# Starting attention inside the last gate pair, and taking bias and gate weights ready-made from DRAM

## The chip, the cores and the metric

The kernel runs on one core of a Trainium2 chip. The metric is the device time of one execution in microseconds, as the median over several runs. The engines are TensorE (PE, with its weight loads shown as PEld), VectorE (DVE), ScalarE (ACT), GpSimd (POOL), and SyncE (SP), whose queue issues every DMA of this kernel.

## The reference

One layer of a hybrid encoder on 1024 rows of width 1024, all in float32:

```
h  = x @ w_in                                   # q, k, v for two head groups, and two gates
ya = chunk_band_attention(qa, ka, va, rel_bias) @ w_proj_a   # 8 softmax heads, band of 9 chunks
yb = stick_breaking_attention(qb, kb, vb) @ w_proj_b         # 8 heads, sigmoid and running products
mix = (sigmoid(ga + b_gate_a) * ya + sigmoid(gb + b_gate_b) * yb) @ w_out
x = layer_norm(alpha * x + mix)
g, u = split(x @ w_ffn_in)
x = layer_norm(alpha * x + (silu(g) * u) @ w_ffn_out)
```

In the softmax heads a score gets a bias that depends on the clipped distance of row and column: on a block of 128 rows by 640 columns, every row has the same list of values, shifted by one place from row to row ("skewed").

## The kernel before

Every float32 factor is split into a high and a low part of a faster matmul type (`split`: a ScalarE cast, then a VectorE subtraction), and a product is three matmuls: high by high, high by low, low by high. A tile is 128 x 1024; its store or load moves 512 KB.

**The order of work.** First the plain products of pair 0 and gate 10. Then the *pairs*: two 128-column blocks of `w_in` are multiplied together by a scheme of seven half-size products (`pair_steps`, each 12 matmuls of 128 x 512). Pairs 1 to 7 give q and k and store them to DRAM; then comes the v stage; then pairs 8 to 12 give ten of the sixteen gates, apply the sigmoid and store them (`out_g`). `run_pairs` walks through the seven steps j = 0 to 6 of each pair, and after a step loads and prepares the weights of later pairs (`right`, `left`) and calls `also`, where side work is placed by hand: the operands of the later output projection (`wo_right`, twelve parts of loads, sums, splits and stores) and the split of the y projection's weights (`proj_weights`), all kept in DRAM until needed.

Then **attention**: 16 heads (0 to 7 softmax, 8 to 15 stick-breaking) with eight rows of blocks each. A row is scores on TensorE into a `sc` bank, then VectorE, ScalarE and GpSimd on the weights (`soft_block`, `stick_block`); later a value step transposes them (`turn`), splits them, and multiplies by v (`mult`). `LEAD` says how many rows are begun ahead of each value step; the first six rows of head 0 begin before its first value step. Between these steps *fillers* keep TensorE busy (`fill_all`, `FILL` per head): the 48 matmuls each of gates 11 to 15, then the 192 of the products yA = y x w_proj_a. Gates 12 to 15 have their weights loaded and split at that time (`load_gate`, cast on ScalarE, subtraction on GpSimd at line 557). While gate 15 runs, `load_y` loads y0 to y3, high and low, into `xt` tiles that held x's parts `xh` and `xl`. Gate 15 takes first all eight k for the low half of the rows, then all eight for the high half. Gates 11 to 15 get their sigmoid only when they are read back (`reload_gate`).

`small_inputs` writes the reversed and padded bias table to `rel_dr`; `rel_bias_tile` reads it skewed into a tile and negates and reverses it on ScalarE (line 652).

After attention come the yB products, the output projection, the norm, and the feed-forward part in the same seven-product scheme.

**What sets the order of instructions.** A scheduler orders each engine's instructions by program order and by when it expects them to be ready, so a filler that is ready may stand ahead of work that waits for a load. Each engine then runs its list strictly in that order. Tiles come from small groups: `cycle(QK, ...)` takes `qs`, `kh` and `kl` in turn, two tiles each (six in all), which also hold q and k of the heads; `gt` has 3, `kp` 4, `op` 8, `xt` 16. Banks: `mm` 2, `sc` 2, `tr` 3, `pv` 1.

Of the kernel before, what the change touches and what calls it, by code (L numbers as in the profile page):

```python
# [18 lines left out]
P = 128  # L19
# [31 lines left out]
def hybrid_trunk_kernel(ctx: ExitStack, tc, x, xt, w_in, w_v, b_gate, rel_bias, w_proj,  # L51
# [54 lines left out]
    pa_dr = [[dr.tile([P, 1024], F32, name=f"pa_dr{i}{p}") for p in "hl"] for i in range(4)]  # L106
    left_dr = {(p, i): dr.tile([P, HW], F32, name=f"left_dr{p}_{i}")
               for i in range(NP2) for p in ORDER}
    rel_dr = dr.tile([8, 896], F32, name="rel_dr")
# [72 lines left out]
    def pair_steps(nm, W, ops, c, done, xtag="mm"):  # L182


        st = {}

        def begin(key, tag, p):
            st[key] = bank(tag, f"{key}{nm}")
            product(st[key], W, ops, p, True)

        def add(dst, src):
            nc.vector.tensor_tensor(dst, src, dst, ALU.add)  # L192

        def p1():
            begin("sx", xtag, 1)
            nc.scalar.copy(c("11"), st["sx"])

        def p2():
            begin("sy", "sc", 2)
            add(c("11"), st["sy"])  # L200
            done("11", None)

        def p6():
            product(st["sx"], W, ops, 6, False)
# [138 lines left out]
    def project(i):  # L343
        kind, pair = work[i][:2]
        tl = {}

        def tile_of(side):
            if side not in tl:
                tl[side] = cycle(QK, f"c{side}_{i}")
# [14 lines left out]
        def out_g(side):  # L364
            gate_sigmoid(tl[side], 2 * pair + int(side) - 1)
# [10 lines left out]

        return pair_steps(f"p{i}", Wa[i], ops_x, c, done)

    def run_pairs(lo, hi, first, also):
# [150 lines left out]

    def proj_weights(cc):

        raw = cycle(QK, f"pa_raw{cc}", F32R)
        hi = cycle(QK, f"pa_hi{cc}", F32R)
        for j, cs in enumerate((LO, HI)):
            load_then(raw[:, cs].bitcast(F32), w_proj[2 * cc + j][:, 0:HW])
        split(hi, raw, raw.bitcast(F32))
        for d, t in zip(pa_dr[cc], (hi, raw)):
            dma(d, t.bitcast(F32))
# [24 lines left out]

    def gate(i, w, gt=None):
# [16 lines left out]
    for _ in gate(first_gate, gate_w, cycle(QK, "gate0")):  # L582
        pass
    first_gate += 1
    wo_at = {(4, 6): 0, (5, 6): 1, (6, 6): 2, (8, 2): 3, (8, 6): 4, (9, 2): 5, (9, 6): 6,
             (10, 2): 7, (10, 6): 8, (11, 2): 9, (11, 6): 10, (12, 2): 11}

    def also(i, j):
# [4 lines left out]
        if i > N_QK and j == 4:  # L593
            proj_weights(i - N_QK - 1)
# [6 lines left out]
    run_pairs(N_QK, len(work), 0, also)  # L601
    first_w = load_gate(first_gate, nc.vector)
# [43 lines left out]
    def rel_bias_tile(head):  # L646
        braw = slot("kp", f"braw{head}")
        src = rel_dr[head:head + 1, 0:640]
        dma(braw[:, 0:640],
            bass.AP(tensor=src.tensor, offset=src.offset, ap=[[1, P], [1, 640]]))  # L650
        bias = slot("kp", f"bias{head}")
        nc.scalar.activation(bias[:, 0:640], braw[:, 0:640][:, ::-1], AF.Copy, scale=-1.0)  # L652
# [150 lines left out]
    def load_proj(cc):  # L803

        parts = []
        for p, d in zip("hl", pa_dr[cc]):
            t = slot("op", f"w{p}_y{cc}", F32R)
            dma(t.bitcast(F32), d)
            parts.append(t)
        return parts  # L810


# [53 lines left out]
    load_qk(heads[0])  # L866
    load_qk(heads[1])
    load_v(heads[0])
    for hd, hidx, g, st, pos, box in vsteps:
# [5 lines left out]
        def begin_rows():  # L875
            begun = state.setdefault("rows", 0)
            upto = min(hidx * 8 + LEAD[hd["br"]][pos], len(wunits))
            for n in range(begun, upto):
                wunits[n]()
            state["rows"] = max(begun, upto)  # L880

        if pos == hidx == 0:
            begin_rows()
# [4 lines left out]
        begin_rows()  # L888
# [493 lines left out]
```

## Time and profile before

| | us |
|---|---|
| median of three runs | 1431.96 (1430.93, 1431.96, 1436.22) |
| profiled execution | 1438.71 |
| its span, first to last instruction | 1436.9 |
| TensorE busy in it | 1405.3 |
| VectorE, ScalarE, GpSimd busy | 1024.1, 689.4, 309.9 |
| q and k pairs | about 43 to 182 |
| v stage | about 182 to 253 |
| gate pairs 8 to 12 | about 253 to 349 |
| first scores of head 0, of head 8 | 356.9, about 472 |
| yA's first products | 549.5 |

Times in the trace are microseconds from the start of the span. A busy TensorE is counted with the tail of each matmul: one of 128 x 512 shows as about 0.39 us, while in a stream they start about 0.23 us apart; so gaps under some 0.17 us do not show as idle. The page's list of DMAs gives bytes and time to landing. The waits list names what ended the idle time of an engine.

### The profile page before, as it was taken

Reading aid. Unit: us, or ns where it says so; the run is one execution under the profiler, and the core shown is the slowest. Engines: PE = TensorE matmul, PEld = TensorE weight load, DVE = VectorE, ACT = ScalarE, POOL = GpSimd, SP = SyncE. Lnnn points to the kernel's source line nnn. Section 1 sums busy time; section 2 is a strip of 40 time slices with the busy share of each in tenths; the row PEclk is TensorE's granted clock in tenths of the full one; section 3 lists DMA queues with packets and bytes.
Section 4 is the critical chain, followed back from the end, with each engine's and each line's share of the span. In section 5 each row is a group of like instructions: output and inputs, shape, how many; then the busy total and the mean of one; then the engine's idle time right before and its main releaser. Section 6 shows DMA issues by size and latency. Waiting matters only on the chain.

```text
span 1436.9 us, 18884 instructions
## 1 busy us (share of the span) xinstructions
PE 1405.3 (98%) x6592; PEld 1159.7 (81%) x6592; DVE 1024.1 (71%) x1596; ACT 689.4 (48%) x1203; POOL 309.9 (22%) x365
## 2 busy tenths in 40 slices
PE   8999999999999998999999999999999999999997
PEld 6888888888778787888888878888888888888886
DVE  8866467773887987897779995555555544785996
ACT  6444354554888876783233543333333332444540
POOL 0000000000565775771303031111111100300012
PEclk9999999999999999999999999999999999999999
DMA  7565737888787559888862143223322227853521
GB/s 249 169 179 181 234 91 275 300 320 302 201 234 226 168 161 278 269 269 301 312 236 85 69 139 125 94 104 110 110 87 91 95 100 251 316 192 110 174 81 73
DMA packets 102895, 264.49 MB, mean 184 GB/s; under 512 B 10880, under 2 KB 27264, under 8 KB 102800
## 3 DMA queue, kind: packets, MB, share of 16 engines
q1 hardware_dynamic: 102800, 263.29, 55.3%
q8 instruction: 52, 0.85, 0.2%
q14 instruction: 43, 0.35, 0.1%
HBM read 172.25 MB, written 90.99 MB: 183 GB/s over the span
## 4 chain that ended last, share of the span: by engine, by line
PE 83%; DVE 8%; DMA 3%; ACT 3%; issue 2%; POOL 1%; POOLq 0%; SPq 0%; DVEq 0%; ACTq 0%
PE dn L1275 15%; PE sxf L179 14%; PE sxp L179 8%; PE szf L179 6%; PE v L431 5%; PE ops L1134 5%; PE szp L179 4%; PE gps L572 4%; PE syf L179 4%; PE yAps L793 2%; PE syp L179 2%; PE tp_b L730 2%; PE tp_a L730 1%; DMA wRf<-in_w_ffn_in_dram 1%; DMA yh<-y_dr2h 1%
## 5 line engine op out<-in xcount | busy, mean ns | idle before, releaser
L1275 PE MATMUL dn<-dr,dl 128*128 128x512 f32 x924 | 209.6, 389 | 0.0
L1275 PEld LDWEIGHTS dn<-dr,dl 128*128 128x128 f32 x924 | 173.4, 188 | 36.0
L704 POOL TENSOR_TENSOR w_b<-w_b,kp_b 128x511 f32<-128x511 f32 (+3 forms) x96 | 103.8, 1085 | 53.0 <-DVE kp_b L701 49.5
L701 DVE TENSOR_TENSOR_SCAN kp_b<-kp_b,ident_ps 128x512 f32<-128x512 f32 (+3 forms) x96 | 92.7, 966 | 4.0 <-ACT kp_b L699 1.4
L112 ACT CAST dl<-raw 128x512 fp32r<-128x512 f32 x77 | 47.5, 623 | 84.7 <-PE dn L1275 68.6
L1134 PE MATMUL ops<-wr,wl 128*128 128x512 f32 x336 | 78.8, 392 | 0.0
L971 POOL TENSOR_TENSOR mv<-mv,neghalf 128x1 f32<-128x1 f32 x16 | 25.6, 1603 | 242.0 <-DVE mv L970 242.0
L1134 PEld LDWEIGHTS ops<-wr,wl 128*128 128x128 f32 x336 | 62.5, 188 | 12.5
L653 POOL MEMSET bias<- 64x64 f32 x8 | 1.2, 146 | 330.1 <-ACT bias L652 330.1
L113 DVE TENSOR_TENSOR dl<-raw,dl 128x512 fp32r<-128x512 f32 x77 | 53.3, 699 | 24.8 <-ACT dl L112 24.2
L674 POOL TENSOR_SCALAR w_a<-w_a,st_a 128x640 f32<-128x640 f32 (+2 forms) x64 | 46.6, 734 | 75.9 <-PE sc_a L634 38.5
L113 DVE TENSOR_TENSOR pt_b<-tp_b,pt_b 128x512 fp32r<-128x512 f32 (+1 forms) x80 | 49.9, 630 | 16.7 <-ACT pt_b L112 15.8
L112 ACT CAST pt_b<-tp_b 128x512 fp32r<-128x512 f32 (+1 forms) x80 | 44.2, 554 | 36.6 <-PE tp_b L730 36.2
L1072 POOL TENSOR_TENSOR sb<-h 128x512 f32<-128x512 f32 x10 | 20.2, 2021 | 185.6 <-PE syf L179 135.1
L179 PE MATMUL szf<-x1S63h,wcf 128*128 128x512 f32 x168 | 55.1, 389 | 0.0
L192 DVE TENSOR_TENSOR gt<-sxf,gt 128x512 f32<-128x512 f32 x21 | 14.4, 686 | 54.9 <-PE sxf L179 54.9
L671 ACT ACTIVATE w_a<-w_a,st_a 128x640 f32<-128x640 f32 (+2 forms) x64 | 44.7, 699 | 13.2 <-DVE st_a L666 11.8
L699 ACT ACTIVATE kp_b<-sc_b 128x512 f32<-128x512 f32 (+3 forms) x96 | 49.0, 511 | 1.5 <-PE sc_b L634 1.4
L700 ACT ACTIVATE w_b<-sc_b 128x511 f32<-128x511 f32 (+3 forms) x96 | 49.1, 512 | 0.0
L1073 POOL TENSOR_TENSOR sa<-h,h 128x512 f32<-128x512 f32 x10 | 15.9, 1586 | 143.0 <-PE sxf L179 120.3
L730 PEld LDWEIGHTS tp_b<-ident,w_b 128*128 128x128 f32 x288 | 36.6, 141 | 12.1 <-issue 1.0
L730 PE MATMUL tp_a<-ident,w_a 128*128 128x128 f32 x240 | 41.9, 277 | 4.4 <-POOL w_a L674 2.5
(1525 smaller groups left out, 4188.2 us busy)
## 6 DMA issues: line engine op xcount, KB each, us to landing
raw<-left_dr SPq DMA_DIRECT2D x77, 256.0 KB, 2.9
wo_dr<-wo SPq DMA_DIRECT2D x28, 512.0 KB, 3.9
wr<-wo_dr SPq DMA_DIRECT2D x28, 512.0 KB, 8.7
wLf<-in_w_ffn_in_dram SPq DMA_DIRECT2D x22, 512.0 KB, 4.4
wRf<-in_w_ffn_in_dram SPq DMA_DIRECT2D x22, 512.0 KB, 4.3
rows<-in_w_ffn_out_dram SPq DMA_DIRECT2D x22, 512.0 KB, 6.3
left_dr<-h SPq DMA_DIRECT2D x33, 256.0 KB, 2.0
v_dr<-vst SPq DMA_DIRECT2D x16, 512.0 KB, 3.2
```

The costliest lines, as they stand in the source:

```text
L112: nc.scalar.copy(dst_h, src)
L113: nc.vector.tensor_tensor(dst_l, src, dst_h.bitcast(F32), ALU.subtract)
L179: mm(acc, lw[:, ks], rx, start=(first and kt == i == 0), stop=(kt == 3 and i == 2), skip_group_check=not first)
L431: mm(banks[mt], xs[lw][:, ms], o[:, rx], start=(fresh and kt == n == 0), stop=(kt == 3 and n == 2), skip_group_check=not fresh)
L572: mm(acc, lw[:, ks], rx[k][:, cs], start=(k == j == 0), stop=(k == KT - 1 and j == 2))
L699: nc.scalar.activation(kp[:, c0:e], sc[:, 0:n], AF.Sigmoid, scale=-1.0)
L700: nc.scalar.activation(be[:, m0:e], sc[:, m0 - c0:n], AF.Sigmoid)
L701: nc.vector.tensor_tensor_scan(kp[:, c0:e], kp[:, c0:e], ident_ps()[:, 0:n], kp[:, c0 - 1:c0] if c0 else 0.0, ALU.mult, ALU.bypass if c0 e ...
L704: nc.gpsimd.tensor_tensor(be[:, m0:e], be[:, m0:e], kp[:, m0 - 1:e - 1], ALU.mult)
L730: tr(tp[:, j:j + P], wt[qb - q0][:, (kb - qb) * P:(kb - qb + 1) * P], ident)
L1134: mm(acc, lw, rx, start=(fresh and n == m == 0), stop=(n == 3 and m == 2), skip_group_check=not fresh)
L1275: mm(acc, lw, rx, start=(fresh and steps[s][1] == n == 0), stop=(last and n == 2), skip_group_check=not fresh)
```

## The change

- *The last gate pair* (pair 12, `final`) leaves `run_pairs` and stands at the start of attention. Its product 2 moves to the sixth place, its bank for that product from `sc` to `tr`, its result tiles from the q/k tiles to `gt`; its two gates (8 and 9) are stored without sigmoid and get it in `reload_gate`. After its step 0 gate 11's weights are loaded, after step 1 q and k of head 0; rows 0 to 2 of head 0 begin after step 4, rows 3 and 4 after step 5, row 5 after step 6.
- *The side work* of the gate pairs is placed anew, so that all of it stands within pairs 8 to 11.
- *The weights of gates 12 to 15* are split during pairs 3 to 6 and kept in DRAM; attention loads the two parts.
- *The bias*: `small_inputs` writes a negated table and from it eight DRAM tables of 128 equal rows; a head's tile is one skewed read, with no ScalarE step, and one `kp` tile in place of two.
- *Gate 15* takes each k through both halves, in two banks at once, and y0 to y3 are loaded after its matmuls 7, 13, 19 and 25, not 28, 31, 34 and 37.

```diff
-    def pair_steps(nm, W, ops, c, done, xtag="mm"):
+    def pair_steps(nm, W, ops, c, done, xtag="mm", ytag="sc", p2_at=1):
...
-            begin("sy", "sc", 2)
+            begin("sy", ytag, 2)
...
-        return [p1, p2, p6, p5, p7, p3, p4]
+        order = [p1, p6, p5, p7, p3, p4]
+        order.insert(p2_at, p2)
+        return order
...
-        nc.vector.tensor_copy(rel_sb[:, 383:896], rel_in[:, ::-1])
-        nc.vector.tensor_copy(rel_sb[:, 0:383], rel_in[:, 512:513].to_broadcast([8, 383]))
+        nc.vector.tensor_scalar(rel_sb[:, 0:384], rel_in[:, 129:513], -1.0, None, ALU.mult)
+        nc.vector.tensor_copy(rel_sb[:, 384:768], rel_sb[:, 383:384].to_broadcast([8, 384]))
         dma(rel_dr, rel_sb)
+        for head in range(8):
+            src = rel_dr[head:head + 1, :]
+            dma(skew_dr[head], bass.AP(tensor=src.tensor, offset=src.offset,
+                                       ap=[[0, P], [1, 768]]))
...
+                tl[side] = slot("gt", name) if final else cycle(QK, name)
...
-            gate_sigmoid(tl[side], 2 * pair + int(side) - 1)
+            if not final:
+                gate_sigmoid(tl[side], 2 * pair + int(side) - 1)
...
+        if final:
+            return pair_steps(f"p{i}", Wa[i], ops_x, c, done, ytag="tr", p2_at=5)
...
+    def keep_split(name, parts, dst):
+        raw = cycle(QK, f"raw_{name}", F32R)
+        hi = cycle(QK, f"hi_{name}", F32R)
+        for cs, src in parts:
+            load_then(raw[:, cs].bitcast(F32), src)
+        split(hi, raw, raw.bitcast(F32))
+        for d, t in zip(dst, (hi, raw)):
+            dma(d, t.bitcast(F32))
+    def gate_weights(i):
+        keep_split(f"g{i}", [(slice(0, D), gate_src(i))], gw_dr[i])
+    def load_split(name, src):
+        parts = []
+        for p, d in zip("hl", src):
+            t = slot("op", f"w{p}_{name}", F32R)
+            dma(t.bitcast(F32), d)
+            parts.append(t)
+        return parts
...
+    def last_gate(i, w):
+        gt = slot("gt", f"gate{i}")
+        accs = [bank("mm", f"gps{i}_{hf}") for hf in range(2)]
+        for k in range(KT):
+            ks = slice(k * P, (k + 1) * P)
+            for acc, cs in zip(accs, (LO, HI)):
+                for j, (lw, rx) in enumerate(((w[0], xh), (w[0], xl), (w[1], xh))):
+                    mm(acc, lw[:, ks], rx[k][:, cs], start=(k == j == 0),
+                       stop=(k == KT - 1 and j == 2))
+                    yield 1.0
+        for acc, cs in zip(accs, (LO, HI)):
+            nc.scalar.copy(gt[:, cs], acc)
+        dma(g_dr[i], gt)
...
-    wo_at = {(4, 6): 0, (5, 6): 1, (6, 6): 2, (8, 2): 3, (8, 6): 4, (9, 2): 5, (9, 6): 6,
-             (10, 2): 7, (10, 6): 8, (11, 2): 9, (11, 6): 10, (12, 2): 11}
+    wo_at = {(4, 6): 0, (5, 6): 1, (6, 6): 2, (8, 0): 3, (8, 3): 4, (8, 6): 5, (9, 2): 6,
+             (9, 5): 7, (10, 1): 8, (10, 4): 9, (11, 0): 10, (11, 3): 11}
+    pa_at = {(8, 5): 0, (9, 4): 1, (10, 2): 2, (10, 6): 3}
...
-        if i > N_QK and j == 4:
-            proj_weights(i - N_QK - 1)
+        if (i, j) in pa_at:
+            proj_weights(pa_at[i, j])
+        if 3 <= i < 7 and j == 4:
+            gate_weights(i + 9)
...
-    run_pairs(N_QK, len(work), 0, also)
-    first_w = load_gate(first_gate, nc.vector)
+    final = len(work) - 1
+    run_pairs(N_QK, final, 0, also, 1)
...
-        braw = slot("kp", f"braw{head}")
-        src = rel_dr[head:head + 1, 0:640]
-        dma(braw[:, 0:640],
-            bass.AP(tensor=src.tensor, offset=src.offset, ap=[[1, P], [1, 640]]))
         bias = slot("kp", f"bias{head}")
-        nc.scalar.activation(bias[:, 0:640], braw[:, 0:640][:, ::-1], AF.Copy, scale=-1.0)
+        src = skew_dr[head][0:1, 127:767]
+        dma(bias[:, 0:640],
+            bass.AP(tensor=src.tensor, offset=src.offset, ap=[[767, P], [1, 640]]))
...
-            nxt = load_gate(i + 1, nc.gpsimd) if i < 15 else load_proj(0)
-            for n, unit in enumerate(gate(i, w)):
-                if i == 15 and n in (28, 31, 34, 37):
-                    load_y((28, 31, 34, 37).index(n))
+            nxt = load_split(f"g{i + 1}", gw_dr[i + 1]) if i < 15 else load_split("y0", pa_dr[0])
+            for n, unit in enumerate(gate(i, w) if i < 15 else last_gate(i, w)):
+                if i == 15 and n in (7, 13, 19, 25):
+                    load_y((7, 13, 19, 25).index(n))
...
-        if 2 * c + br >= 2 * N_GATE:
+        if 2 * c + br >= 2 * N_GATE - 2:
             gate_sigmoid(t, 2 * c + br)
...
-    load_qk(heads[0])
+    for j, step in enumerate(project(final)):
+        step()
+        also(final, j)
+        if j == 0:
+            first_w.extend(load_gate(first_gate, nc.vector))
+        if j == 1:
+            load_qk(heads[0])
+        if j >= 4:
+            rows_to((3, 5, 6)[j - 4])
     load_qk(heads[1])
     load_v(heads[0])
```

More of the change, by code (lines that the diff above doesn't have):

```diff
@@ L106, in hybrid_trunk_kernel @@
     pa_dr = [[dr.tile([P, 1024], F32, name=f"pa_dr{i}{p}") for p in "hl"] for i in range(4)]
+    gw_dr = {i: [dr.tile([P, 1024], F32, name=f"gw_dr{i}{p}") for p in "hl"]
+             for i in range(12, 16)}
     left_dr = {(p, i): dr.tile([P, HW], F32, name=f"left_dr{p}_{i}")
                for i in range(NP2) for p in ORDER}
-    rel_dr = dr.tile([8, 896], F32, name="rel_dr")
+    rel_dr = dr.tile([8, 768], F32, name="rel_dr")
+    skew_dr = [dr.tile([P, 768], F32, name=f"skew_dr{i}") for i in range(8)]
     def split(dst_h, dst_l, src):
@@ L344, in project @@
         kind, pair = work[i][:2]
+        final = i == len(work) - 1
         tl = {}
@@ L348, in tile_of @@
             if side not in tl:
-                tl[side] = cycle(QK, f"c{side}_{i}")
+                name = f"c{side}_{i}"
+                tl[side] = slot("gt", name) if final else cycle(QK, name)
             return tl[side]
@@ L375, in done, with run_pairs @@
                 out("2")
+        if final:
+            return pair_steps(f"p{i}", Wa[i], ops_x, c, done, ytag="tr", p2_at=5)
         return pair_steps(f"p{i}", Wa[i], ops_x, c, done)
-    def run_pairs(lo, hi, first, also):
+    def run_pairs(lo, hi, first, also, ahead=0):
         steps = {i: project(i) for i in range(lo, hi)}
@@ L387, in run_pairs @@
                 p()
-                if j == 0 and i + 1 < hi:
+                if j == 0 and i + 1 < hi + ahead:
                     right(i + 1)
-                if j == 1 and lo + 2 <= i + 2 < hi and i + 2 >= lo + first:
+                if j == 1 and lo + 2 <= i + 2 < hi + ahead and i + 2 >= lo + first:
                     left(i + 2)
@@ L529, in wo_right @@
             put(4, b[:, LO])
-    def proj_weights(cc):
[L533 to L539, printed above, removed]
+    def keep_split(name, parts, dst):
[6 more added lines that the diff above has]
+            dma(d, t.bitcast(F32))
+    def proj_weights(cc):
+        keep_split(f"pa{cc}", [(cs, w_proj[2 * cc + j][:, 0:HW])
+                               for j, cs in enumerate((LO, HI))], pa_dr[cc])
+    def gate_weights(i):
[7 more added lines that the diff above has]
+        return parts
     def load_w(srcs, name, raw, hl, lo_eng):
@@ L768, in value_steps @@
         return steps
+    first_w = []
     def fill_all():
@@ L780, in fill_all @@
         for cc in range(4):
-            nxt = load_proj(cc + 1) if cc < 3 else None
+            nxt = load_split(f"y{cc + 1}", pa_dr[cc + 1]) if cc < 3 else None
             if cc:
@@ L801, in fill_all @@
             w = nxt
[L803 to L810, printed above, removed]
     KEEP, kept = 5, {}
@@ L865, in hybrid_trunk_kernel, with rows_to @@
     goal = 0.0
-    load_qk(heads[0])
+    def rows_to(upto):
+        for n in range(state.get("rows", 0), upto):
+            wunits[n]()
+        state["rows"] = max(state.get("rows", 0), upto)
+    for j, step in enumerate(project(final)):
[7 more added lines that the diff above has]
+            rows_to((3, 5, 6)[j - 4])
     load_qk(heads[1])
@@ L874, in hybrid_trunk_kernel @@
             load_v(heads[hidx + 1])
[L875 to L883, printed above, removed]
         if st == 0:
@@ L887, in hybrid_trunk_kernel @@
         turn()
-        begin_rows()
+        rows_to(min(hidx * 8 + LEAD[hd["br"]][pos], len(wunits)))
         last = goal
```

2 lines of the change are left out of this document (1 added, 1 removed).

## The prediction

> **What bounds the kernel now.** I read the page first (its busy times and clock), then the stages as windows, then the waits of TensorE, then the timeline and the chain of waits where TensorE stops.
>
> ```profile
> PE 1405.3 (98%) x6592; PEld 1159.7 (81%) x6592; DVE 1024.1 (71%) x1596; ACT 689.4 (48%) x1203; POOL 309.9 (22%) x365
> ```
>
> TensorE is the bound, and no matmul is added or taken away. The span is 1436.9 us, so at most 31.6 us (1436.9 - 1405.3) of plain idle time can be won, plus slow-clock time and short gaps that count as busy.
>
> ```profile
> 43.00:182.00 139.00, 139.00 (x612) 114.11 (x611) 87.21 (x112) 60.02 (x82) 0.00 (x0) 1.00 0.65 195
> 253.00:329.00 76.00, 75.76 (x334) 62.40 (x333) 54.07 (x74) 43.87 (x62) 0.29 (x2) 1.00 0.84 305
> 329.00:349.00 20.00, 20.00 (x90) 16.53 (x90) 7.47 (x10) 9.41 (x13) 0.00 (x0) 1.00 0.89 331
> 355.00:380.00 25.00, 22.02 (x124) 17.17 (x123) 16.75 (x64) 17.67 (x39) 11.33 (x18) 1.00 0.79 215
> 380.00:476.00 96.00, 92.55 (x569) 77.00 (x568) 81.00 (x261) 81.17 (x188) 54.73 (x88) 1.00 0.75 214
> 535.00:550.00 15.00, 15.00 (x86) 12.85 (x85) 13.66 (x17) 12.86 (x30) 11.96 (x22) 1.00 1.01 304
> 550.00:565.00 15.00, 10.13 (x48) 8.41 (x47) 7.59 (x10) 6.58 (x16) 4.77 (x6) 0.77 1.00 328
> ```
>
> The columns are busy us and count of TensorE, its weight loads, VectorE, ScalarE and GpSimd, then clock, DMA share, GB/s. The pair stages (43 to 182, 253 to 349) lose nothing, so whatever the change puts there is free only as long as that holds. The change aims at three losing stretches: the start of attention (355 to 380), the softmax heads (380 to 476), and 550 to 565, where the clock falls as well.
>
> **Part 1: y's loads.** Gate 15 runs just before the yA products, which need y0 to y3 (eight transfers of 512 KB).
>
> ```profile
> 538.73 0.38 SPq L819 DMA_DIRECT2D yh<-y_dr0h  x1
> 540.64 0.35 SPq L819 DMA_DIRECT2D yl<-y_dr1l  x1
> ...
> 549.70 0.32 SPq L819 DMA_DIRECT2D yl<-y_dr3l  x1
> ...
> SPq L819 <- DMA yh<-y_dr1h: 2.6, 1, 2.6
> ...
> 525.00:530.00 5.00, 5.00 (x31) 4.28 (x30) 4.37 (x6) 3.50 (x9) 3.46 (x7) 1.00 0.10 38
> 530.00:535.00 5.00, 5.00 (x31) 4.34 (x30) 3.76 (x6) 3.87 (x10) 2.87 (x3) 1.00 0.32 86
> ...
> 526.82 0.40 PE L572 MATMUL gps<-xl,wh_g 128*128 128x512 f32 x1
> ...
> 536.44 0.39 PE L572 MATMUL gps<-xl,wh_g 128*128 128x512 f32 x1
> ...
> 542.71 0.40 PE L572 MATMUL gps<-xh,wl_g 128*128 128x512 f32 x1
> ...
> 553.61 0.33 PE L744 MATMUL pv_b<-pt_b,v 128*128 128x256 f32 x1
> 558.64 0.80 PE L793 MATMUL yAps<-yh,wh_y 128*128 128x512 f32 x1 [4.70 <-DMA yh<-y_dr2h]
> ...
> 562.01 0.63 PE L793 MATMUL yAps<-yl,wh_y 128*128 128x512 f32 x1
> 562.44 0.55 PE L793 MATMUL yAps<-yh,wl_y 128*128 128x512 f32 x1
> 562.82 0.39 PE L793 MATMUL yAps<-yh,wh_y 128*128 128x512 f32 x1
> 563.05 0.39 PE L793 MATMUL yAps<-yl,wh_y 128*128 128x512 f32 x1
> ```
>
> The y loads can start only when gate 15's second half lets x's tiles go, and then crowd into 11 us with the DMAs already at share 1.01; SP even waits for the first of them to land before it issues the last. The first yA products run, and the seventh waits 4.70 us for y2h. Then matmuls start 0.43 us apart (562.01, 562.44), where 0.23 is the pace (562.82, 563.05). From 558.64 to 562.82, 4.2 us at about half speed cost 2.1. Together 6.8 us.
>
> After, gate 15 takes each k through both halves, so each xh/xl pair falls free every 6 matmuls. Do the loads at its matmuls 7, 13, 19, 25 find free tiles? Were tiles reused strictly in turn, y1l would take xh3, which the row at 542.71 still reads; it issued at 540.64. So a load takes whichever tile fell free first, and eight are free by matmul 24. The matmuls numbered 7 and 25 ran at 526.82 and 536.44, so the loads issue between 527 and 537, over 12 us earlier than the last one did (549.70), into a stretch in which the DMAs moved 38 and 86 GB/s. Value: **-6.8**, bounds -7.5 and -3 (the reload of gA, or head 12's q and k in the same queue, could become the late one). Gate 15 now holds both `mm` banks at once; at its ends a copy of 0.6 us stands close to the next use: counted below.
>
> The Trainium skill ("TensorE: Matmul & The Clock Gate", Part 1) says the clock is halved after an idle window of some 3.4 us; the rows at 562 agree (0.43 against 0.23). By its rule a leftover wait under 3.4 us would cost only itself.
>
> **Part 2: the start of attention.**
>
> ```profile
> 340.54 2.72 PE sxp L179 x12
> ...
> 348.70 8.39 PE gps L572 x37
> ...
> PE tp_a L730 <- POOL w_a L674: 1.6, 3, 1.1
> PE tp_a L730 <- DVE pt_a L113: 0.8, 1, 0.8
> ...
> 345.57 0.89 SPq L617 DMA_DIRECT2D kl<-k_dr  x1
> ...
> 351.39 0.84 SPq L617 DMA_DIRECT2D kl<-k_dr  x1
> ...
> 356.92 0.45 PE L633 MATMUL sc_a<-kh,qs 128*128 128x320 f32 x2
> ```
>
> While q and k of head 0 are on their way (its k loads stand from 345.57 to 351.39, the first score at 356.92), TensorE uses up 37 of gate 11's 48 filler matmuls; when the rows start there is little left to fill with, and 355 to 380 loses 25 - 22.02 = 2.98 us idle. At the later pace (569 in 96 us, 0.169 us each) 25 us would hold 148 matmuls, not 124: 4.0 us short. After, q and k load during the last pair, whose c tiles no longer sit in their slots, rows 0 to 5 run over its products 2 and 4 (5.4 us), and the 37 matmuls fill heads 0 to 2. Value **-2.5**, bounds 0 (the gaps move on with the next rows) and -4.
>
> What it puts into the last pair: ten score cuts of two matmuls. If TensorE's order keeps the first six together, two banks at VectorE's pace hold it: about 0.6 us a cut (486 ns, in the group below, plus its read-out) against 0.3 of matmuls, some 2 us at most; before, matmuls of the gate were mixed between the scores. With the bank changes of gate 15 and two gates' sigmoids moved to their reload (1.15 us of ScalarE each, L341 below): **+0.5**, bounds 0 and +2.5.
>
> **Part 3: prepared bias and weights.** It takes out of the softmax heads:
>
> ```profile
> L652 ACT ACTIVATE bias<-braw 128x640 f32<-128x640 f32 x7 | 5.2, 741 | 0.9 <-DMA braw<-rel_dr 0.9
> L548 ACT CAST wh_g<-wr_g 128x1024 fp32r<-128x1024 f32 x3 | 3.1, 1049 | 0.2 <-DMA wr_g<-in_w_in_dram 0.2
> L557 POOL TENSOR_TENSOR wl_g<-wr_g,wh_g 128x256 fp32r<-128x256 f32 x12 | 9.4, 820 | 0.3 <-ACT wh_g L548 0.3
> L666 DVE CUSTOM_DVE_ANT_0 w_a<-sc_a,bias 128x320 f32<-128x320 f32 (+2 forms) x64 | 31.0, 486 | 19.2 <-PE sc_a L634 15.3 <-POOL bias L654 3.2 <-PE sc_a L633 0.2
> ```
>
> 8.3 us of ScalarE, 9.4 of GpSimd, 3.2 of VectorE's waits for a bias. None of it is TensorE's own time; the stage loses 96 - 92.55 = 3.45 us idle to such chains, in gaps of well under 1 us, and more in gaps too short to show. Value **-2.0**, bounds 0 and -5. The bias tile now waits for its DMA without ScalarE between; that drops 0.74 us, and one `kp` slot of two, a head.
>
> The work comes back in pairs 3 to 6: four times a cast and a subtraction as these,
>
> ```profile
> L113 DVE TENSOR_TENSOR pa_raw<-pa_raw,pa_hi 128x1024 fp32r<-128x1024 f32 x4 | 4.9, 1218 | 0.3 <-ACT pa_hi L112 0.3
> ...
> L341 ACT ACTIVATE c<-c,bg 128x1024 f32<-128x1024 f32 x9 | 10.4, 1154 | 5.2 <-DVE c L192 5.1
> ...
> L112 ACT CAST pa_hi<-pa_raw 128x1024 fp32r<-128x1024 f32 x4 | 4.2, 1048 | 0.7 <-DMA pa_raw<-in_w_proj_dram 0.7
> ```
>
> (pa_raw and pa_hi; the row between them is a gate's sigmoid) beside 87 and 60 busy us of 139: hidden. Its DMA is 4 x 1.57 MB, and the eight skewed tables write 8 x 0.39 MB: 9.4 MB on 27 MB (195 GB/s x 139 us), a share of 0.65 rising to about 0.88. What queues behind the eight table writes on SP is q and k stores, whose tiles ScalarE needs, and weight loads with a pair (19 us) in hand. **+0.3**, bounds 0 and +3.
>
> **Part 4: the gate pairs.** All remaining w_out parts and w_proj splits move ahead of the last pair, into pairs 8 to 11. In transfers of 524 KB: a pair needs 4 (two weight loads, two gate stores); a w_out part 4, 3 or 2; a w_proj split 3. Pair 8: 4+4+3+3+2 = 16, or 8.39 MB; pair 9: 14, 7.34; pair 10: 16, 8.39; pair 11, which loads one weight tile fewer: 8, 4.19. Together 28.3 MB in 4 x 7 x 2.72 = 76.2 us, 371 GB/s. Before, 305 at a share of 0.84 and 331 at 0.89 put a full share at 363 to 372. At 368, pairs 8 and 10 need 22.8 us each for their 19.0, pair 9 19.9: 8.5 us behind at the end of pair 10, of which pair 11 (11.4 for 19.0) makes up most.
>
> ```profile
> 272.00:291.00 19.00, 18.76 (x83) 15.17 (x82) 13.46 (x19) 11.17 (x16) 0.00 (x0) 1.00 0.90 332
> ...
> 277.47 6.02 DMA woraw<-in_w_out_dram
> ```
>
> Behind a late w_out or w_proj load stand ScalarE and VectorE, in order, and behind them the copies that free a bank: TensorE has two to five products (5.4 to 13.6 us) before it stops. A 6.02 us wait cost 0.24 us (19 - 18.76). With 8.5 against 5.4, 3 us at one place; I take **+2.0**, bounds 0 and +8.5. The Trainium skill ("DMA: Bandwidth & Descriptors", Specifications) gives some 358 GB/s from HBM to a core. By that figure 28.3 MB take 79.1 us, an estimate that speaks against the change; the 363 to 372 drawn from the trace lies just above it.
>
> **Sum:** -6.8 - 2.5 + 0.5 - 2.0 + 0.3 + 2.0 = **-8.5 us**. The profiled execution took 1438.71 us (span 1436.9 and 1.8 around it), so 1430.2 by it; it is 6.75 us above the median of the three runs, 1431.96, and I carry the difference over whole: **1423.5 us**. About 0.5% (7.2 us: 1424.8 to 1439.1) is what a measurement of this kernel tells from no change.
>
> **Rivals.**
> A. *As summed*: 1419 to 1429, chance 0.52, of which 0.10 lies above 1424.8.
> B. *The gate pairs become DMA-bound* (slower). If the DMAs carry no more than the 305 GB/s which 253 to 329 moved, 28.3 MB take 92.8 us in place of 76.2, 16.6 us late; with the other terms (-10.5) that is +6.1, 1438. Below 301 GB/s (17.7 us late) it ends slower by over 0.5%, at 1440 or more. For it: weights, w_out and stores share one SP queue and six tiles. Against: 331 at share 0.89. Slower 0.15, a tie 0.06.
> C. *The stall at y is smaller in plain runs than in the profiled one*, whose 6.75 us over the median are about the stall's 6.8. Then only the rest is left, -1.7: 1430. Against: the loads' crowding is in the program. 0.10.
> D. *Deeper gain*: with ScalarE and GpSimd relieved and fillers in place, parts 2 and 3 reach their bounds (-9 for -4.5), and the gate pairs cost nothing: 1417. 0.12.
> E. *Rows too early*: q and k of head 0 not landed when product 3 ends. They are asked for after product 6, three products (8.2 us) before the first row; if they take the 11.4 us from 345.57 to 356.92 again and the scores stand ahead of product 2, TensorE waits 3.2 us: 1426.7. 0.05.
>
> Faster 0.42 + 0.12 = 0.54; same 0.10 + 0.06 + 0.10 + 0.05 = 0.31; slower 0.15. Range 1413 to 1434: D with its spread below, A, C, E and the ties of B inside; B's slower part stays outside.
>
> **What would show it.** Part 1: y loads issued before 540, no wait of yAps for y, clock 1.00 throughout. Part 2: first score during the last pair, and the filler spread over heads 0 to 2. Part 3: L652 gone, fewer waits of tp_a for w_a. Part 4: TensorE idle in pairs 8 to 11, none or a few us. Wrong if those pairs idle by 10 us, or if a new wait stands at yA.

## The result, and the profile after

The changed kernel takes **1444.35 us** (median of 5, 1443.2 to 1446.56) against 1431.66 for the kernel before (median of 5): a ratio of 1.0086 [1.0067, 1.0105], 12.7 us slower where 8.5 less were forecast. Its profiled execution took 1444.35 us too. The loss stands where the prediction had put 0.3 us: in pairs 1 to 7.

The page, and three of the windows shown before (busy us and count of TensorE, its loads, VectorE, ScalarE, GpSimd; clock; DMA share; GB/s), of the changed kernel:

```profile
PE 1405.6 (97%) x6592; PEld 1159.0 (80%) x6592; DVE 1029.9 (71%) x1600; ACT 684.0 (47%) x1195; POOL 294.0 (20%) x349
```

```profile
43.00:182.00 139.00, 129.04 (x547) 103.48 (x546) 87.45 (x109) 59.17 (x77) 0.00 (x0) 0.98 0.74 233
329.00:349.00 20.00, 17.35 (x69) 13.75 (x68) 13.30 (x19) 9.34 (x14) 0.00 (x0) 0.91 0.83 317
550.00:565.00 15.00, 15.00 (x87) 12.71 (x86) 13.12 (x18) 12.00 (x28) 11.45 (x19) 1.00 0.99 304
```

From 43 to 182 TensorE was never idle before (x612); now it does 65 matmuls fewer, at the same busy time of VectorE and ScalarE (87.45 and 59.17, before 87.21 and 60.02) and with DMAs that are busier, 0.74 for 0.65, but far from full. From 329 to 349 it loses time in the last gate pair. The stall at 550 to 565 is gone. The softmax heads lose less; they all run some 12 us later now, so they are compared from first score to first score: from head 0 to head 8 TensorE is idle for 2.5 us (118.80 - 116.34), before for 5.8 (114.90 - 109.07). The first matmuls of pairs 1 and 8, of the changed kernel and then of the kernel before:

```profile
L182 PE MATMUL syp<-xh,wlp1h x4: 389/389/389, 42.9 to 44.9; 128*128 128x512 f32 x4
L182 PE MATMUL sxp<-xh,wlp8h x4: 389/389/389, 267.7 to 269.7; 128*128 128x512 f32 x4
```

```profile
L179 PE MATMUL syp<-xh,wlp1h x4: 389/389/389, 42.7 to 44.7; 128*128 128x512 f32 x4
L179 PE MATMUL sxp<-xh,wlp8h x4: 389/389/389, 252.8 to 254.8; 128*128 128x512 f32 x4
```

So pairs 1 to 7 with the v stage ("pairs 1-7" below) take 224.8 us, not 210.1: **14.7 us lost**. Some 10 of them are plain idle time of TensorE, and 4.7 lie in matmuls that follow each other more slowly (the same 926 matmuls are busy for 214.84 us, before 210.10). How it comes about the first time is seen in the timelines of SP, VectorE and TensorE, with two waits of the changed kernel below them; then SP's timeline of the kernel before:

```profile
86.27 6.22 SPq L314 DMA_DIRECT2D skew_dr<-rel_dr  x8
92.59 0.54 SPq L322 DMA_DIRECT2D q_dr<-c  x1
...
96.29 0.37 SPq L137 DMA_DIRECT2D raw_g<-in_w_in_dram  x1
99.48 0.45 SPq L321 DMA_DIRECT2D k_dr<-hi  x1
...
104.30 0.36 SPq L553 DMA_DIRECT2D gw_dr12h<-hi_g  x1
...
111.94 1.09 SPq L137 DMA_DIRECT2D wRp<-in_w_in_dram  x1
...
123.14 0.68 DVE L157 TENSOR_TENSOR tap<-wRp,wLp 128x512 f32<-128x512 f32 x1
...
128.84 0.50 PE L182 MATMUL szp<-s13h,wap5h 128*128 128x512 f32 x1 [4.01 <-ACT wap5h L115]
131.41 0.63 PE L182 MATMUL szp<-s13h,wap5h 128*128 128x512 f32 x1
131.84 0.63 PE L182 MATMUL szp<-s13l,wap5h 128*128 128x512 f32 x1
...
ACT c L199 <- DMA gw_dr12h<-hi_g: 2.8, 1, 2.8
PE szp L182 <- ACT wap6h L115: 2.0, 1, 2.0
```

```profile
88.66 0.60 SPq L134 DMA_DIRECT2D wRp<-in_w_in_dram  x1
...
99.07 0.46 SPq L312 DMA_DIRECT2D k_dr<-hi  x1
```

The eight skew writes take SP 6.22 us to issue, and the q stores come behind them. More than these 6 us is lost by the order of SP's list. In the kernel before the right weights of pair 5 (`wRp`) are issued at 88.66, ahead of the next eight q and k stores. In the changed kernel they stand behind these eight stores, and behind the gate's load and its two stores, for the first of which SP waits until ScalarE has cast it (104.30): they are issued at 111.94, 23 us later. Why the scheduler built this order is not shown. ScalarE, too, waits 2.8 us, for a tile that the gate's store holds. VectorE, in order, takes the weights up at 123.14, behind the late end of pair 4, and TensorE stands 4.01 us for them and then starts matmuls 0.43 us apart for a while (131.41, 131.84), in place of 0.23. The next pair repeats it (wap6h).

### The profile page after: what moved, and what is told of

Read it like the earlier page. It is cut to its first block, busy times and chain, and to the rows that moved or that the text cites. A ratio compares the mean times of both kernels' runs of the same rounds, so it can differ in the third digit from the quotient of the medians.

```text
span 1442.5 us, 18876 instructions
## 1 busy us (share of the span) xinstructions
PE 1405.6 (97%) x6592; PEld 1159.0 (80%) x6592; DVE 1029.9 (71%) x1600; ACT 684.0 (47%) x1195; POOL 294.0 (20%) x349
## 4 chain that ended last, share of the span: by engine, by line
PE 82%; DVE 9%; DMA 4%; ACT 2%; issue 2%; POOL 1%; SPq 0%; POOLq 0%; DVEq 0%; ACTq 0%
PE sxf L182 15%; PE dn L1317 15%; PE szf L182 7%; PE sxp L182 7%; PE v L445 5%; PE ops L1176 5%; PE syf L182 4%; PE szp L182 3%; PE gps L616 3%; PE yAps L840 2%; PE tp_b L775 2%; PE syp L182 1%; PE tp_a L775 1%; PE pv_b L790 1%; PE sc_b L680 1%
## 5 line engine op out<-in xcount | busy, mean ns | idle before, releaser
L1114 POOL TENSOR_TENSOR sb<-h 128x512 f32<-128x512 f32 x10 | 15.4, 1539 | 184.7 <-PE syf L182 134.5
L716 ACT ACTIVATE w_a<-w_a,st_a 128x640 f32<-128x640 f32 (+2 forms) x64 | 44.5, 697 | 13.6 <-DVE st_a L711 12.4
L775 PEld LDWEIGHTS tp_b<-ident,w_b 128*128 128x128 f32 x288 | 35.8, 140 | 12.4 <-DVE pt_b L116 1.0
L116 DVE TENSOR_TENSOR dr<-rows,dr 128x512 fp32r<-128x512 f32 x66 | 44.5, 682 | 0.8 <-ACT dr L115 0.7
```

The costliest lines, as they stand in the source:

```text
L116: nc.vector.tensor_tensor(dst_l, src, dst_h.bitcast(F32), ALU.subtract)
L775: tr(tp[:, j:j + P], wt[qb - q0][:, (kb - qb) * P:(kb - qb + 1) * P], ident)
```

## The experiments

"Pairs 1-7" is from the first matmul of pair 1 to that of pair 8, "to head 8" from there to the first score of head 8, both in the profiled run. Ratios are to the kernel before in the same session, whose medians were 1430.8 to 1432.8. The first theory was that pairs 1 to 7 lose to the two preparations of part 3, and that the kernel before has no stall at y in most runs. Its rivals were that one preparation costs it all, and that the gate pairs do.

| run | us | ratio | pairs 1-7 | to head 8 |
|---|---|---|---|---|
| before (profiled) | 1438.7 | | 210.1 | 219.0 |
| after | 1444.35 | 1.0086 [1.0067, 1.0105] | 224.8 | 216.0 |
| e1 y only | 1432.5 | 0.9998 [0.9988, 1.0008] | 210.1 | 218.3 |
| e2 no gate weights | 1439.4 | 1.0045 [1.0030, 1.0060] | 216.5 | 218.7 |
| e3 no skew | 1437.3 | 1.0037 [1.0024, 1.0050] | 216.4 | 216.0 |
| e4 neither | 1430.8 | 0.9990 [0.9980, 0.9999] | 210.3 | 217.8 |
| e5 before again | 1430.4 | | 210.2 | 218.5 |
| e6 = e4, y3 split at use | **1427.3** | **0.9963 [0.9951, 0.9976]** | 210.1 | 212.8 |
| e7 = e2, skew in v stage | 1432.6 | 1.0002 [0.9993, 1.0011] | 210.1 | 217.4 |
| e11 = e2, skew by GpSimd | 1432.4 | 0.9989 [0.9978, 0.9999] | 210.2 | 215.3 |
| e8 (time), e15 (profile) = e4, copies by SP | 1446.3 | 1.0097 [1.0082, 1.0113] | 224.3 | 217.4 |
| e12 = e4, copies by GpSimd | 1450.1 | 1.0113 [1.0092, 1.0135] | 210.4 | 216.0 |
| e9 = e3, v tiles | 1441.7 | 1.0065 [1.0053, 1.0078] | 218.7 | 217.9 |
| e10 = e3, by GpSimd | 1439.3 | 1.0041 [1.0026, 1.0056] | 219.7 | 218.0 |
| e13 = e3, both | 1443.0 | 1.0078 [1.0063, 1.0092] | 221.8 | 219.2 |
| e14 = e13, y3 at use | 1436.6 | 1.0038 [1.0024, 1.0051] | 220.9 | 212.2 |
| e16 = e14, skew by GpSimd | 1434.9 | 1.0029 [1.0020, 1.0039] | 220.6 | 211.0 |
| e17 = e14, early loads | 1430.3 | 0.9985 [0.9976, 0.9993] | 213.4 | 212.4 |
| e18 = e17, skew by GpSimd | 1443.6 | 1.0070 [1.0057, 1.0084] | 229.0 | 211.9 |

**Parts of the change.** e1 is the kernel before with `last_gate` and the earlier y loads alone; e2 to e4 take preparations out of the changed kernel.

```diff
 e2, e4:
-        if 3 <= i < 7 and j == 4:
-            gate_weights(i + 9)
 e3, e4: small_inputs and rel_bias_tile as before
```

> The kernel before with one part of the change: gate 15 takes each k through both halves and y0 to y3 load after its matmuls 7, 13, 19 and 25. In the profiled execution of before the stall at yA cost 6.8 us, but that execution was 7 us above the plain runs. Theory (the stall is mostly not there in plain runs): the plain median stays within 2 us of before, 1430 to 1432, though the trace has no wait of yAps for y. Rival (the stall is in every run): 1425, 6 to 7 us less. Either way the y loads issue before the trace's yA by 12 us or more.

> The changed kernel, but gates 12 to 15 load and split their weights in attention as before (ScalarE cast, GpSimd subtraction), so pairs 3 to 6 do no gate weights. Between v's end and the pairs the changed kernel lost 15 us in pairs 4 to 7. Theory T (the gate weights' two tiles of the six q/k tiles, held until their stores land, and their place in the in-order queues): 10 to 13 of the 15 us go, softmax heads lose 2 again; about 1434. Rival S (the eight skewed table writes, which push the q and k stores back): pairs 4 to 7 still lose 12 or more; 1444 to 1446. Rival B (both together, either alone is harmless): about 1432.

> The changed kernel, but the bias is made as before (one reversed table, skewed read, ScalarE reversal and negation). Theory T: pairs 4 to 7 still lose 11 us or more; 1441 to 1446. Rival S: they lose under 4 us; about 1433. Rival B: about 1432.

> The changed kernel without the gate weights of pairs 3 to 6 and without the skewed tables: what is left is the last pair at the start of attention, the new places of the side work in the gate pairs, and y. Pairs 4 to 7 should lose nothing (v ends at 252 to 254 us); the gate pairs still lose some 5 us at pair 12 (weights behind a late w_proj load); softmax heads gain 2 less than in the changed kernel. All theories: 1431 to 1434, that is the whole 12 us lies in the two preparations of part 3. If it is above 1438, the moved pair itself costs more than the trace shows.

Each preparation alone costs 6.1 to 6.2 us in pairs 1 to 7, both together 14.5 (224.8 - 210.3): no one of them is the culprit. With neither, the rest of the change is worth 1.2 us by medians, barely clear of nothing by its interval. In e1 the stall at y is gone from the trace (span 1430.0, profiled before 1436.9), yet its median is that of the kernel before.

**The stall at y.** So the kernel before was profiled once more, unchanged.

> The kernel before, run and profiled once more. Theory (the stall at y belongs to some executions only): span 1429 to 1431 us, head 8 to head 12 in 83.2 us as in every other trace, no wait of yAps for y above 1 us. Rival (every execution of the kernel before has the stall, and something else of 6 us differs between the profiled one and the others): the wait of some 4.7 us stands at yAps again, and head 8 to head 12 takes 88.4 us.

Its span was 1428.5 us. The window, and the last y load of SP's timeline, of this run:

```profile
550.00:565.00 15.00, 14.76 (x88) 12.53 (x86) 12.72 (x18) 11.01 (x27) 9.24 (x15) 1.00 1.04 365
...
545.42 0.32 SPq L819 DMA_DIRECT2D yl<-y_dr3l  x1
```

The same program issued its last y load at 545.42 and TensorE did not wait for y; in the first profile it was 549.70, with a stall of 4.7 us. Of 25 runs beside e1 to e4 two took 1437 us or more and the others 1430.0 to 1433.8: the stall belongs to few executions. (Those two were not profiled; that they had it is inferred.)

**The gate pairs.** In e6 the last of w_proj's four splits leaves pair 10, and y3's weights are split where they are used.

```diff
-    pa_at = {(8, 5): 0, (9, 4): 1, (10, 2): 2, (10, 6): 3}
+    pa_at = {(8, 5): 0, (9, 4): 1, (10, 2): 2}
...
+                nxt = load_w([(cs, w_proj[6 + j][:, 0:HW]) ...], "y3", of("op"), of("op"), nc.gpsimd)
```

> The version with neither the prepared gate weights nor the skewed table (1430.8 us), and y3's weights are no longer split ahead of the last gate pair: they are loaded raw and split at their use, as the gates' weights are. Theory (gate pairs too full): the DMAs are what makes pair 12's right weights late; without 1.6 MB there (one load and two stores of 1 MB) the wait of 2.7 us in pair 12 and the slow clock behind it go, and the time falls by about 4.5 us to 1426.5 (1425.5 to 1428). Rival 1 (another load takes its place, pairs 8 to 11 stay at the DMAs' limit): 1429 to 1431. Rival 2 (splitting y3's weights in the heads costs there what is won here): pair 12 runs without a wait, but the stretch from head 8 to head 12 grows from 83.2 us by 1 us or more; 1428 to 1430.

Waits from 310 on and the first matmuls behind them in e4, and then the window from 329 to 349 in e6 (pair 12 starts at 321.6 there):

```profile
PE sxp L179 <- ACT wbp12h L112: 2.7, 1, 2.7
ACT hi_pa L112 <- DMA raw_pa<-in_w_proj_dram: 2.4, 1, 2.4
...
329.47 0.62 PE L179 MATMUL sxp<-s24h,wbp12h 128*128 128x512 f32 x1 [2.66 <-ACT wbp12h L112]
329.89 0.63 PE L179 MATMUL sxp<-s24l,wbp12h 128*128 128x512 f32 x1
```

```profile
329.00:349.00 20.00, 20.00 (x93) 16.55 (x91) 7.67 (x13) 8.13 (x11) 0.29 (x2) 1.00 0.82 255
```

ScalarE stood for w_proj's load, pair 12's weights came late, and TensorE lost 2.7 us and some more at half clock. Without that load 5.0 us come back (217.8 to 212.8), and y3's split costs nothing that shows. It runs from 589.5 to 595.1, behind the stretch that the expectation had named (head 8 to head 12, 83.2 us in both); from head 8 to the first yB product e6 takes 185.9 us and e4 185.0, while the other profiles of the table, but for the first of the kernel before with its stall at y, lie between 184.7 and 186.4. e6 is the fastest kernel of all: 1427.3 us.

**The skewed bias.** In e7 its eight writes stand in the v stage, in e11 GpSimd issues them where they stood.

```diff
 e7:  v_load(1, ...)
+     skew_tables()
 e11:
-            dma(skew_dr[head], ...)
+            nc.gpsimd.dma_start(skew_dr[head], ...)
```

> The changed kernel without the prepared gate weights (1439.4 us), with the eight writes of the skewed bias moved from pair 2 into the stage of the values, where the queue of SP stands empty for some 18 us. Theory (place, not table: the writes stand ahead of q and k stores in SP's queue and hold the tiles that ScalarE waits for): pairs 1 to 7 take 210 to 211.5 us again instead of 216.5, and the time is 1432.5 to 1434. Rival (the loss comes with the skewed bias itself, its reads or its tiles): 1438 to 1440, with the loss in the same place or in the heads.

> The changed kernel without the prepared gate weights (1439.4 us), with the eight writes of the skewed bias still in pair 2 but issued by GpSimd. Theory of the queue: SP goes on with the q and k stores at once, pairs 1 to 7 take 210.3 to 212 us, total 1432 to 1434. Theory of bytes (3.1 MB at one place fill the DMAs for some 8 us, and all that is issued in them lands late): 214 to 217 us, total 1437 to 1440.

Both give pairs 1 to 7 back whole: the place on SP's queue costs, not the table. The queues of e11 from 80 to 100 us, and how long its q stores and the right weights of pair 5 take from issue to landing; then the q stores of the changed kernel; then SP's timelines of e2 (two rows) and of e11 (one):

```profile
q1 hardware_dynamic: 842, 2.78, 46.8%
q0 software_dynamic: 506, 2.54, 40.4%
...
q_dr<-c SPq DMA_DIRECT2D x2, 256.0 KB, 6.4
wRp<-in_w_in_dram SPq DMA_DIRECT2D x1, 512.0 KB, 12.8
```

```profile
q_dr<-c SPq DMA_DIRECT2D x2, 256.0 KB, 8.0
```

```profile
94.40 0.45 SPq L320 DMA_DIRECT2D q_dr<-c  x1
...
109.49 1.13 SPq L135 DMA_DIRECT2D wRp<-in_w_in_dram  x1
```

```profile
88.51 1.15 SPq L135 DMA_DIRECT2D wRp<-in_w_in_dram  x1
```

The tables' bytes are the same; but in e11 the q stores start at 86.02 beside the tables, in the changed kernel at 92.59 behind them. And the weights of pair 5 keep their old place in e11 (88.51) and in e7 (88.52), while in e2 they are issued at 109.49, behind eight more stores, though SP had nothing to issue from 94.85 to 99.44. In e11 they took 12.8 us to land (5.1 in e4), and nothing was lost: a late landing had slack, the late place had none. Whether the writes could stay on SP in pair 2, tied behind these loads, was not run. The Trainium skill ("DMA: Bandwidth & Descriptors", Queues, rings and completion order) says that a DMA engine takes turns between its queues; the two shares, 46.8% and 40.4%, agree.

**The gates' weights.** Of what a preparation takes (two q/k tiles, SP's order, a cast and a subtraction, bytes), single things were taken away. First bytes alone: three copies a pair, from DRAM to DRAM, tied on SP behind the last weight load (`issue_after`).

```diff
+    def gate_copies(i):
+        with tc.issue_after(last_load[0]):
+            for t in gw_dr[i]:                      # three DRAM tiles
+                dma(t, gate_src(i))                 # e12: nc.gpsimd.dma_start
...
-            gate_weights(i + 9)
+            gate_copies(i + 9)
```

> The version with neither preparation (1430.8 us), and in each of pairs 3 to 6 three DRAM to DRAM copies of 512 KB, as many bytes and issues on SP as the preparation of a gate's weights has, but no tile, no cast and no subtraction (the copies are read by nobody). Theory of tiles (the two q/k tiles that a gate's weights hold for a load, a cast, a subtraction and two stores are what pairs 3 to 6 lack): pairs 1 to 7 take 210.3 to 212 us, total 1430.5 to 1433. Theory of traffic (SP's queue or the DMAs' share alone): 214 to 217 us, total 1435 to 1438.

> The version with twelve DRAM to DRAM copies issued by SP in pairs 3 to 6, once more, for a profile at full clock (1446.3 us in its plain runs, 15.4 above the version without them). Theory (copies ahead of q and k stores and weight loads in the same queue make these land late, so that ScalarE waits for a q/k tile and VectorE for a weight): pairs 1 to 7 take some 225 us, with waits of ScalarE for stores or of VectorE for weights of several us. Rival (the loss stands outside pairs 1 to 7): those take 210 to 213 us.

> The version with twelve DRAM to DRAM copies of 512 KB in pairs 3 to 6 (1446.3 us from SP), issued by GpSimd instead. They wait for nothing and hold nothing, so only the transfers themselves are left. Theory of the queue: 1430.5 to 1433 us, pairs 1 to 7 in 210.3 to 212.5 us. Theory of bytes: 1440 to 1448 us, pairs 1 to 7 in 220 us or more.

Without tile, cast or subtraction the copies on SP cost 14.0 us (224.3 - 210.3), more than twice the 6.1 of the preparation that they stand for: tiles are not needed for a loss, so they are not shown to be its cause. The copies are no clean measure of the bytes either, for SP's list changes again: pair 5's right weights are issued at 106.53 and pair 7's at 156.33, where e4 has 88.42 and 126.53. In e12 GpSimd's queue held nothing back, as its timeline and the first matmul of pair 1 show:

```profile
1.28 0.71 POOL L557 DMA_DIRECT2D gw_dr12h<-in_w_in_dram  x1 [0.32 <-issue]
...
L181 PE MATMUL syp<-xh,wlp1h x4: 389/389/389, 60.8 to 62.8; 128*128 128x512 f32 x4
```

All twelve copies were issued by 13.8 us, among the first loads, and pair 1 began at 60.8 us in place of 42.5; the run tells nothing of pairs 3 to 6.

Then the preparation itself, with other tiles, another queue, or both:

```diff
 e9, e13:
-        raw = cycle(QK, f"raw_{name}", F32R)
+        raw = slot("v", f"raw_{name}", F32R)      # hi too; pairs 1 to 3
 e10, e13:
-            dma(d, t.bitcast(F32))
+            nc.gpsimd.dma_start(d, t.bitcast(F32))  # the load too
```

> The changed kernel without the skewed table (1437.3 us), with the preparation of gates 12 to 15 done in the two v tiles, which nobody uses before pair 4's end, in pairs 1 to 3, instead of in q and k's six tiles in pairs 3 to 6. All its loads, casts, subtractions and stores stay. Theory of tiles: pairs 1 to 7 take 210.3 to 212 us instead of 216.4, and the softmax heads keep their gain of 1.8, so 1429 to 1431.5. Theory of traffic or of ScalarE's and VectorE's order: 214 to 217 us, total 1433 to 1437.

> The changed kernel without the skewed table (1437.3 us), with the load and the two stores of each gate's preparation issued by GpSimd, which is idle in the pairs, instead of SP; tiles, casts, subtractions and bytes stay. Theory of the queue (what costs 6 us in pairs 3 to 6 is order on SP: a weight load stands behind q and k stores and behind a store that waits for ScalarE's cast): pairs 1 to 7 take 210.3 to 212 us, total 1429 to 1431.5. Theory of bytes (the DMAs' full stretches make the weights and stores late, whoever issues): 215 to 218 us, total 1436 to 1438.5.

> The changed kernel without the skewed table (1437.3 us), with both repairs of the gates' preparation at once: the v tiles in pairs 1 to 3 instead of q's and k's, and GpSimd issuing the loads and stores instead of SP. Each alone kept or raised the loss (pairs 1 to 7: 218.7 us with the v tiles, 219.7 us with GpSimd, 216.4 us with neither). Theory of relays (a preparation takes tiles, a place in SP's order and a load that the casts behind it must wait for; with one mended, another takes its place): with tiles and queue free together pairs 1 to 7 take 210.3 to 212 us, and with 1.8 us won in the heads the total is 1428.5 to 1431. Rival (2 MB of weights loaded and 4 MB stored in the pairs are too many bytes, or the cast and subtraction in ScalarE's and VectorE's order are enough): 214 to 220 us, total 1434 to 1440.

None helps, and each fails at another place. e9, SP's timeline and a wait:

```profile
108.53 0.59 SPq L316 DMA_DIRECT2D q_dr<-hi  x1
113.64 0.33 SPq L548 DMA_DIRECT2D gw_dr15h<-hi_g  x1
...
117.68 1.17 SPq L136 DMA_DIRECT2D wRp<-in_w_in_dram  x1
...
PE szp L181 <- ACT wap5h L114: 3.8, 1, 3.8
```

SP stands till 113.64 for a gate's cast, and the weights of pair 5 come behind it. e10, waits from 140 to 185:

```profile
ACT hi_g L114 <- DMA raw_g<-in_w_in_dram: 3.6, 1, 3.6
ACT c L198 <- DMA gw_dr15l<-raw_g: 3.1, 1, 3.1
PE sxp L181 <- ACT c L198: 5.7, 2, 4.5
```

ScalarE stands for the gate's load and then for the tile that its store holds; the copy that frees a bank is late. e13, ScalarE's and TensorE's timeline:

```profile
85.50 1.05 ACT L114 CAST hi_g<-raw_g 128x1024 fp32r<-128x1024 f32 x1 [7.51 <-DMA raw_g<-in_w_in_dram]
...
93.24 0.79 PE L181 MATMUL sxp<-s24h,wbp3h 128*128 128x512 f32 x1 [4.78 <-ACT c L198]
```

Here the gates have tiles and a queue of their own, yet ScalarE stands 7.51 us before a cast whose load was issued only at 79.38: with two v tiles it had to wait until a store of the gate before had freed one. So e13 took the q/k tiles out of the matter, but not every wait for a tile. e14 and e16 add the other mends:

> The same with y3's weights split at their use, as in the version that ran in 1427.3 us. If the theory of relays holds, both gains add: 1424.5 to 1427. If the gates' preparation still costs 4 us or more, 1430 to 1434.

> The whole change with its three placements mended: gates' weights prepared in the v tiles and issued by GpSimd, the skewed bias written by GpSimd, y3's weights split at use. If each mend takes away its own loss and the skewed bias brings nothing by itself: 1424.5 to 1428, pairs 1 to 7 in 210.3 to 212 us. If three streams on GpSimd's queue collide: pairs 1 to 7 in 214 us or more, 1430 to 1436.

They add as far as they should (e14 to head 8: 212.2), but the loss in pairs 1 to 7 stays above 10 us. e17 takes the last thing away: raw weights are loaded one or two pairs ahead into the v tiles, and each cast is tied behind a copy of its pair.

```diff
+    def gate_store(i):
+        raw, hi = raws[i], cycle(QK, f"hi_g{i}", F32R)
+        with tc.issue_after(anchor[0]):
+            split(hi, raw, raw.bitcast(F32))
```

> No skewed table, y3's weights split at use (1427.3 us without prepared gate weights, 1436.6 us with them in the v tiles by GpSimd). Here the gates' raw weights take the two v tiles and are loaded by GpSimd one to two pairs before their cast, and each cast stands on ScalarE behind a named copy of its pair; the upper half goes to one q/k tile for its store. Theory (ScalarE in its order stands up to 7.5 us before a cast whose load was issued just before, and the copy behind it keeps a bank from TensorE): pairs 1 to 7 take 210.3 to 212.5 us, the heads keep 1.8, total 1425 to 1428. Rival (six more transfers and two more passes per gate are too much for pairs 1 to 4 wherever they stand): 214 to 221 us, total 1430 to 1437.

> The same with the skewed bias, whose eight writes GpSimd issues: the whole change with its placements mended. If the skewed bias costs and brings nothing: within 1.5 us of the run without it, 1425 to 1428. If its writes on GpSimd's queue, which now come behind the gates' stores, collide with pairs 3 and 4: pairs 1 to 7 in 213 us or more, 1429 to 1433.

7.5 us come back (220.9 to 213.4) with every byte, cast and subtraction still there. 3.1 are left; waits and a row of e17:

```profile
ACT c L209 <- DMA k_dr<-hi: 6.9, 1, 6.9
...
77.29 0.50 PE L181 MATMUL sxp<-s13h,wap2h 128*128 128x512 f32 x1 [2.50 <-ACT c L209]
```

Even so placed the preparation does not pay: it brings 0.4 us to head 8 (212.8 in e6, 212.4 in e17), and e17 is slower than e6. e18 shows the relay once more: the skew writes stand ahead of the gates' stores on GpSimd's queue, and a store that comes late holds a q/k tile. Its waits:

```profile
ACT c L201 <- DMA gw_dr15h<-hi_g: 9.1, 1, 9.1
PE sxp L182 <- ACT c L201: 9.5, 1, 9.5
```

ScalarE's wait of 9.1 us for that store becomes 9.5 us in which TensorE stands.

## Why the prediction was wrong

- **The step that failed** is the last of part 3: "beside 87 and 60 busy us of 139: hidden", +0.3 with a bound of +3. It measured +14.7. The DMA share was even below the forecast (0.74, not 0.88, in a stretch that ran slower), and the engines had the time. What I read was busy time; what mattered is order. I named the queue ("q and k stores, whose tiles ScalarE needs, and weight loads with a pair (19 us) in hand") and gave it no price. The pair in hand was there where the loads kept their place in SP's list (e11). In the changed kernel the list has the right weights of pair 5 behind eight more stores: they were issued at 111.94, not 88.66, which is more than the 19 us, and TensorE missed them at 124.8, with the load (about 6 us), VectorE's order and ScalarE's cast in between. No rival covered pairs 1 to 7.
- **Part 1** was right in its mechanism and wrong in its base. The loads were issued about where forecast (524.86 to 539.90 in e1), and neither e1 nor the changed kernel stops at yA. But "I carry the difference over whole" assumed that the stall is in the runs whose median counts. It is in few, as rival C had it, and e5 has none with nothing changed; the term was 0 there. (The load for which SP waited before the last one, `y_dr1h`, was the third, not the first.)
- **Part 2** came out larger: e1 to e6, which differ in it and in what is left of part 4, go from 218.3 to 212.8, 5.5 us for the 2.0 forecast and beyond its bound of 4. TensorE's plain idle time in that stretch fell from 6.1 to 3.6 us; the rest lies in what counts as busy.
- **Part 3's gain** was near its forecast. e4 and the changed kernel differ in the two preparations alone. From the first score of head 0 to that of head 8 they take 120.3 and 118.8 us, at as many matmuls: -1.5 for -2.0. Their windows, e4 first:

```profile
350.20:470.50 120.30, 115.97 (x711) 98.55 (x711) 95.49 (x318) 96.84 (x220) 63.95 (x105) 1.00 0.77 217
```

```profile
364.90:483.70 118.80, 116.34 (x711) 98.76 (x710) 95.87 (x318) 89.01 (x209) 56.21 (x93) 1.00 0.79 231
```

One preparation alone moved this stretch by less than 1 us: the gates' weights by +0.2 (e4 to e3) and -0.8 (e6 to e17), the bias by -0.4 (e4 to e2) and -0.6 (e4 to e11). The 1.8 us by which e3 is shorter than e4 in the table, and on which the expectations of e9, e13 and e17 count, do not come from the heads. They lie before the first score (95.6 us from pair 8 to it, not 97.4): both kernels stop in pair 12, but only in e4 is the stop followed by half clock (shown in the last section).
- **Part 4**: the mechanism as told, a late w_proj load with ScalarE behind it. +5.0 (e6 to e4), where I took +2.0 of 0 to 8.5; the figure left out that a wait of 2.7 us can be followed by half clock.
- **The sum by these terms**: 0 - 5.5 - 1.8 (e4 to the changed kernel, to head 8) + 14.7 + 5.0 = +12.4, measured +12.7. The three terms behind pair 8 are differences along one row of runs, from e1 over e6 and e4 to the changed kernel; that they add up is no test of how they are divided.
- **Rival B** forecast a slower kernel at 1438 or more, but by gate pairs that lose 16.6 us or more. They lost 5.0; that its time is the nearest is luck.

**Open.** That SP's list had moved pair 5's weights is read in the traces; why, was not asked. For the skewed bias e7 and e11 show that with the weights in their old place nothing is lost. For the gates' weights early loads gave back 7.5 of 10.6 us, but what of the last 3.1 us in e17 is tile and what queue was not separated. In these runs the cost goes with lateness, not with the work; they do not give one resource as its cause, since with each one freed the next took over.

## What to carry to other kernels

A stage without idle time has slack only as long as every in-order queue finds its operand there: price moved work by what stands behind its load on ScalarE, SP and VectorE, and who needs the tile it holds, not by busy shares. After such a move, compare when each weight load is issued before and after: here one had slipped by a whole pair. Load well before the cast that needs it, and keep bulk writes off the queue that carries weight loads and stores on which tiles depend. And before a stall of one profiled execution goes into a sum against a median, see that the median has it.

## What the runs showed of the hardware

TensorE's clock fell to half after shorter stops than the prediction had put down, and not by their length. At one place, before pair 12's product with `wbp12h`, e3 stopped 2.61 us and went on at the full pace, and e9 stopped 2.46 us and went on at half of it:

```profile
335.57 0.50 PE L181 MATMUL sxp<-s24h,wbp12h 128*128 128x512 f32 x1 [2.61 <-ACT wbp12h L114]
335.91 0.40 PE L181 MATMUL sxp<-s24l,wbp12h 128*128 128x512 f32 x1
336.14 0.41 PE L181 MATMUL sxp<-s13h,wap11h 128*128 128x512 f32 x1
```

```profile
337.95 0.79 PE L181 MATMUL sxp<-s24h,wbp12h 128*128 128x512 f32 x1 [2.46 <-ACT wbp12h L114]
338.54 0.63 PE L181 MATMUL sxp<-s24l,wbp12h 128*128 128x512 f32 x1
338.97 0.63 PE L181 MATMUL sxp<-s13h,wap11h 128*128 128x512 f32 x1
```

The matmuls are 0.23 us apart in e3 (335.91, 336.14) and 0.43 in e9 (338.54, 338.97). e4 (2.66 us) went the way of e9, e11 (2.59) and e17 (2.50, at another place) that of e3. In e4 eight matmuls ran at half pace, some 1.6 us beside the stop. The Trainium skill ("TensorE: Matmul & The Clock Gate", Part 1) speaks of an idle window of some 3.4 us, and of the window as free-running; here the measurement decides: a stop of 2.5 to 2.7 us can cost more than itself, and whether it does cannot be read off its length alone.

Copies that wait for nothing started at 1.3 us on GpSimd's queue, though they are written into pairs 3 to 6 (e12), and delayed the first pair by 18 us.
